# A transformer layer on one core: weight buffers of the first feed-forward layer and residual loads of the second

## The chip, the cores and the metric

The kernel runs on one NeuronCore of a Trainium2 chip, as one launch. The metric is the device time of that launch in microseconds (us). The kernel before takes 2638.78 us, the median of three runs (2638.66 to 2640.82).

## The reference, cut to what matters

One layer of a streaming encoder in fp32, on 2048 new positions and 8 x 16 further ones, 2176 rows of 1024 in all. A projection feeds a gated convolution and a differential attention; the concatenation goes through an output projection and a layer norm. The change concerns only the last two lines:

```python
x1 = layer_norm(ALPHA * x + einsum('bse,ed->bsd', mixed, w_out), ln1_g, ln1_b)
hdn = square(relu(einsum('bsd,df->bsf', x1, w_ff1)))          # first layer, 1024 -> 4096
y = layer_norm(ALPHA * x1 + einsum('bsf,fd->bsd', hdn, w_ff2), ln2_g, ln2_b)   # second, 4096 -> 1024
```

## The kernel before, in words

**Numbers.** Every fp32 product is made of three passes of a reduced type: an operand is split into a high part (a cast on ScalarE, L64) and a low part (a subtraction on VectorE, L67, or on GpSimd), and `mm3` (L71 to L73) adds high x high, low x high (the names in the trace are stationary, moving) and high x low in PSUM. So each operand that TensorE reads is two tiles, h and l, and comes to be by two instructions on two engines.

**First layer.** A Strassen-Winograd scheme takes 2 x 2 blocks with 7 products in place of 8. The 17 row tiles are in three groups of 5, 6 and 6 tiles; a product then has 320 columns in the first group and 384 in the other two. Per group a loop over 16 pairs of column blocks of w_ff1 (`for p in range(NPAIR)`, L1119): the two weight tiles of the pair are loaded (`load_w1`, each 512 KB, into two of the four buffers "raw"), four sums S1 to S4 are formed of them (`w_sources`: the first on GpSimd, L134, three on VectorE), and seven weight operands (11, S1, 12, S2, S3, 22, S4) are split into h and l (`w1_form`). Each of the seven has a place of its own in the pool w1p, with one buffer. `products` makes the 7 products, each 4 x 3 matmuls, and after each product writes the call that forms the same weight for the next pair: it may begin when that product has left the place free. Results go through six PSUM banks, five per pair, through Relu and Square on ScalarE (L1033, L1034) and a few sums, and are stored as seven forms to `hf` in HBM.

**Side work in groups 1 and 2.** Behind some pairs stands work for the next group. `norm_out` (pairs 2, 4, 6, 8, 10, 12) loads a row tile of x1, normalises it and stores it. `turn_out` (pairs 5, 9, 13) loads two such tiles, transposes them on TensorE through four of the six PSUM banks, forms the seven operands T1 and so on, and stores them with seven DMAs (L1113). Its four work tiles, and norm_out's one, are taken from the same four "raw" buffers as the weights. At the end of a group the seven operands of the next group are loaded (L1140) and split. In the third group, which has no such side work, the odd row tile's second layer runs beside the pairs (`odd_prep`, `odd_step`), with buffers wr (two), w2h and w2l of its own.

**Second layer.** Six passes (`PASSES`, L1211) of 16 chunks; a chunk is 24 matmuls of 512 columns. For each chunk a tile of `hf` is loaded to "raw" (`h_load`, L1164, split on ScalarE and VectorE), and one or two quarters of w_ff2 to the places of S1 to S4 (`w_quarter`, L1178, 256 KB), combined on GpSimd in some passes (L1194 to L1200, T = difference of two quarters in the first pass), then split. `prep` does this three chunks ahead. In passes 0, 1, 2 and 5 the residual is prepared: at p == 2 `begin` loads eight halves of x1 to acc tiles (L1259, 256 KB each), and at p = 4 to 11 `residual` multiplies and adds the first norm's gain and bias to one of them on VectorE (L1265, L1266; not for the first group's tiles, whose x1 is stored complete).

**What sets the order.** The program is written in the order of the text, and a scheduler with a simulated timeline then orders each engine's queue: an instruction may move ahead of others on its queue where its operands and buffers allow it. The DMA issues of loads and of most stores share the queue of the sync engine (SP), in one order; a DMA whose buffer is not free waits in that queue with what stands behind it. `tc.issue_after(i)` keeps a DMA behind instruction i.

Of the kernel before, what the change touches and what calls it, by code (L numbers as in the profile page):

```python
# [18 lines left out]
P = 128  # L19
D = 1024  # L20
# [37 lines left out]
def hybrid_layer(ctx: ExitStack, tc: tile.TileContext, A):  # L58
# [82 lines left out]

    def products(N, psum, tmp, X, W, S, form, out, after=None):

        nxt, banks = {}, {}

        def product(xn):
            wn = dict((x, w) for w, x in PRODUCTS)[xn]
            key = {"21": "11", "22": "T1"}.get(xn, xn)  # L150
            more = key in banks
            if not more:
                banks[key] = psum.tile([P, 512], F32, name="pf")[:, :N]
            ps = banks[key]
            for kt in range(4):
                mm3(ps, W[wn][0][:, kt, :], W[wn][1][:, kt, :], X[xn][0][:, kt, :N], X[xn][1][:, kt, :N],
                    kt == 0 and not more, kt == 3, more)
            if wn in S:
                nxt[wn] = form(S, wn)
            if after is not None:  # L160
                after(xn)
            return ps

        u1, u2 = tmp("u1"), tmp("u2")
        for xn in NAMES:
            ps = product(xn)
            if xn == "11":
                nc.scalar.copy(u1, ps)  # L168
            elif xn == "21":
                out(0, 0, ps, True)  # L170
            elif xn == "T2":
                nc.vector.tensor_add(u1, ps, u1)
            elif xn == "T3":
                nc.vector.tensor_add(u2, ps, u1)
                c = tmp("c")
                nc.vector.tensor_add(c, banks["T1"], u2)  # L176
                out(1, 1, c)
            elif xn == "T4":
                c = tmp("c")
                nc.vector.tensor_sub(c, u2, ps)  # L180
                out(1, 0, c)
            elif xn == "22":
                c = tmp("c")
                pin[:] = [nc.vector.tensor_add(c, ps, u1).ins]
                out(0, 1, c)
        return nxt
# [334 lines left out]
    NPAIR = NF // 2  # L521

    loads = []

    def load_w1(p):
        ra, rb = (rwp.tile([P, KT, P], F32, name="raw") for _ in range(2))
        nc.sync.dma_start(ra, A["w_ff1"][p])
        loads.append(nc.sync.dma_start(rb, A["w_ff1"][p + NPAIR]).ins)
        return w_sources(wsp, ra, rb, nc.vector)

    def w1_form(S, nm):
        hl = [w1p.tile([P, 4, P], F32R, name=f"w{nm}{p}") for p in "hl"]
        split(*hl, S[nm], nc.vector)
        return hl


    with ExitStack() as ph:
# [424 lines left out]
        rwp = ffn.enter_context(pool("rwp", 4, side="right"))  # L962
        w1p = ffn.enter_context(pool("w1p", 1, side="right"))
        xtp = xst.enter_context(pool("xtp", 1, side="right"))
# [23 lines left out]
        for i, t in enumerate(ORDER):  # L988
# [11 lines left out]
            if i == 8:  # L1000
                S, W = load_w1(0), {}
                for wn, _ in PRODUCTS:
                    W[wn] = w1_form(S, wn)
# [4 lines left out]
    with ffn as ph:  # L1008
# [8 lines left out]
        def ff1(n, p, X, W, S, at):  # L1017
# [32 lines left out]

            return products(N, ps_f, tmp, X, W, S, w1_form, out)

        def odd_prep(f):

            raw = w2p.tile([P, D], F32, name="wr", bufs=2)
            with tc.issue_after(loads[-1]):
# [9 lines left out]
        def odd_step(f, banks, h, w):  # L1066
            for half in range(2):
                hs = slice(half * 512, half * 512 + 512)
                mm3(banks[half], *h, w[0][:, hs], w[1][:, hs], f == 0, f == NF - 1)

        def norm_out(t):

            r = rwp.tile([P, D], F32, name="xs", tag="raw")
            nc.sync.dma_start(r, x1d[t])
# [12 lines left out]
        def turn_out(gi, i):  # L1087


            a, b = (rwp.tile([P, D], F32, name="xs", tag="raw") for _ in range(2))  # L1090
            for r, t in zip((a, b), groups[gi + 1][i::3]):
                nc.sync.dma_start(r, x1d[t])
            quads = []
            for r in (a, b):
                for g in range(2):
# [3 lines left out]
                    quads.append(ps)  # L1099
            c, d = (rwp.tile([P, D], F32, name="xs", tag="raw") for _ in range(2))  # L1100
            F = {"11": c[:, :512], "21": c[:, 512:], "22": d[:, :512], "T1": a[:, :512], "T2": a[:, 512:],
# [10 lines left out]
            for nm in NAMES:  # L1112
                nc.sync.dma_start(x1f[gi][nm][:, :, i * P:(i + 1) * P], F[nm].rearrange("p (k t) -> p k t", k=4))  # L1113

        couples = [(g[i], g[i + 3]) for g in groups for i in range(len(g) // 2)]
        odd, base, op_, obanks = groups[0][2], 0, None, None
        for gi, tiles in enumerate(groups):
            n, end = len(tiles), gi + 1 == len(groups)
            for p in range(NPAIR):  # L1119
                last = p == NPAIR - 1  # L1120
                S = {} if last and end else load_w1((p + 1) % NPAIR)
                W = ff1(n, p, X, W, S, base * P)
# [30 lines left out]

        def h_load(pieces):

            raw = rwp.tile([P, D], F32, name="hraw", tag="raw")
            for o, src in pieces:
                n = 1
                for k in src.shape[1:]:
                    n *= k  # L1160
                dst = raw[:, o:o + n]
                if len(src.shape) == 3:
                    dst = dst.rearrange("p (k t) -> p k t", k=src.shape[1])
                nc.sync.dma_start(dst, src)  # L1164
            hl = [hrp.tile([P, D], F32R, name="hr" + q) for q in "hl"]
            split(*hl, raw, nc.vector)
            return hl
# [4 lines left out]

        slot = [0]

        def w_quarter(src):
            slot[0] += 1
            a = wsp.tile([P, 512], F32, name="wq", tag=f"wS{slot[0] % 4 + 1}")
            nc.sync.dma_start(a, src)  # L1178
            return a

        def w_load(p, nm):


            rows = {"1": A["w_ff2"][p + NPAIR], "2": A["w_ff2"][p]}

            def quarter(q):
                return w_quarter(rows[q[0]][:, 512 * (q[1] == "2"):512 * (q[1] == "2") + 512])

            if nm in ("T1", "T3"):
                a = quarter("12" if nm == "T1" else "22")  # L1190
                b = quarter("11" if nm == "T1" else "12")
                if nm == "T1":
# [5 lines left out]
            elif nm in ("T2", "T4"):  # L1198
                a = quarter("22" if nm == "T2" else "21")
                nc.gpsimd.tensor_sub(T[p], a, T[p])  # L1200
                a = T[p]
            else:
                a = quarter(nm)
            wn = PRODUCTS[turn_[0] % len(PRODUCTS)][0]
            turn_[0] += 1
            hl = [w1p.tile([P, 512], F32R, name="v" + q, tag=f"w{wn}{q}") for q in "hl"]
            split(*hl, a, nc.vector)
            return hl

        turn_ = [0]  # L1210
        PASSES = (("S1", "T1", None, 2, 1), ("S4", "22", "go", 1, 1), ("11", "11", None, 1, 0), ("S2", "T2", "go", 1, 1),  # L1211
                  ("S3", "T3", "go", 2, 1), ("22", "T4", "go", 2, 0))
        chunks = [(k, p) for k in range(len(PASSES)) for p in range(NPAIR)]

        def prep(k, p):
            hn, wn = PASSES[k][:2]
            return h_load([(0, hf[p][:, FORMS.index(hn), :])]), w_load(p, wn)

# [7 lines left out]

        LEAD = 3
        ready = [prep(*c) for c in chunks[:LEAD]]
        last_odd = rwp.tile([P, D], F32, name="odd", tag="raw")
# [22 lines left out]

        def begin(r, half):
            for c in couples:
                t = c[2 - r]
                if t not in acc:
                    acc[t] = acp.tile([P, D], F32, name=f"acc{t}")
                hs = slice(half * 512, half * 512 + 512)
                nc.sync.dma_start(acc[t][:, hs], x1d[t][:, hs])  # L1259
# [9 lines left out]
        for n, (k, p) in enumerate(chunks):  # L1269
            if n + LEAD < len(chunks):  # L1270
                ready.append(prep(*chunks[n + LEAD]))
            (hh, hl), (wh, wl) = ready.pop(0)
# [3 lines left out]
            if k in (0, 1, 2, 5):  # L1276
                if p == 2:
                    begin(r, half)
                elif 4 <= p < 12:
                    residual(p - 4, r, half)  # L1280
# [12 lines left out]
        def last_w(p):  # L1293
            a = w_quarter(A["w_ff2"][p][:, :512])
            if p < len(PRODUCTS):
                hl = [w1p.tile([P, 512], F32R, name="v" + q, tag=f"w{PRODUCTS[p][0]}{q}") for q in "hl"]
            else:
                hl = [wrp.tile([P, 512], F32R, name=f"z{p}{q}") for q in "hl"]
# [3 lines left out]
        def last_h(q):  # L1302

            if q < 8:
                return h_load([(512 * k, hf[2 * q + k][:, F12, :512]) for k in range(2)])
            i, e = 4 + (q - 8) // 2, (q - 8) % 2
            return h_load([(P * k, hf[8 * e + k][:, F12, i * P:(i + 1) * P]) for k in range(8)])

# [108 lines left out]
```

## Time and profile before

| | us |
|---|---|
| median of three runs | 2638.78 |
| the profiled execution's own time | 2638.29 |
| its span, first to last instruction | 2636.5 |
| TensorE (PE) busy | 2493.7 (95%) |
| VectorE (DVE) busy | 1870.2 (71%) |
| ScalarE (ACT) busy | 1293.2 (49%) |
| GpSimd (POOL) busy | 933.2 (35%) |

[...] The first layer runs from about 1186 to 1986 us of the span (its first pairs among the end of the output projection), the second from 1991 to the end. Busy time is that in which an engine executes; a stretch with TensorE busy can still be slow where the granted clock is low, so matmuls per stretch are counted beside it.

### The profile page before, as it was taken

How to read it: one execution, taken by the hardware profiler on the slowest of the kernel's cores; microseconds unless marked ns; L12 is line 12 of the kernel's file. 1: busy time of each engine (PE TensorE's matmuls, PEld its weight loads, DVE VectorE, ACT ScalarE, POOL GpSimd, SP SyncE). 2: the span in 40 equal slices, each digit the busy share in tenths (PEclk: the TensorE clock that was granted, in tenths of full speed). 3: DMA queues.
4: the chain of work that ended last, by engine and by line, in shares of the span. 5: the costliest groups of instructions: out<-in, count | busy, mean ns of one | idle time of the engine just before them, and what ended most of it. 6: DMA issues, size and time to landing. Idle time of an engine off the chain costs nothing. (4 is left out here: it accounts for less than half of the span.)

```text
span 2636.5 us, 38836 instructions
## 1 busy us (share of the span) xinstructions
PE 2493.7 (95%) x13420; PEld 2257.5 (86%) x13420; DVE 1870.2 (71%) x3103; ACT 1293.2 (49%) x2676; POOL 933.2 (35%) x778
## 2 busy tenths in 40 slices
PE   8999999989999999999997999899998899999998
PEld 7999999968787877789887998899996688888886
DVE  7797676766867777877877777888877634444478
ACT  5444345346666765336665566656553232222231
POOL 5575654655655554221213222322223301314100
PEclk9999999989999999999998999999999899999999
DMA  7437335364535424545766566756668644546444
GB/s 252 157 112 233 111 103 176 86 184 135 158 118 148 141 94 154 181 144 172 229 213 230 188 224 216 286 189 210 213 224 305 207 144 151 167 131 203 144 149 147
DMA packets 273317, 463.24 MB, mean 176 GB/s; under 512 B 32320, under 2 KB 178832, under 8 KB 273120
## 3 DMA queue, kind: packets, MB, share of 16 engines
q1 hardware_dynamic: 260160, 431.58, 50.6%
q10 hardware_dynamic: 11088, 24.12, 2.4%
q0 software_dynamic: 1872, 5.07, 0.6%
q8 instruction: 105, 1.72, 0.3%
q14 instruction: 92, 0.75, 0.1%
HBM read 316.98 MB, written 143.69 MB: 175 GB/s over the span
## 5 line engine op out<-in xcount | busy, mean ns | idle before, releaser
L71 PE MATMUL y<-vh,hrh 128*128 128x512 f32 x824 | 315.8, 394 | 17.5 <-ACT vh L64 17.5
L72 PE MATMUL y<-vl,hrh 128*128 128x512 f32 x824 | 322.0, 391 | 3.2 <-DVE vl L67 3.2
L73 PE MATMUL y<-vh,hrl 128*128 128x512 f32 x824 | 321.4, 390 | 0.0
L67 DVE TENSOR_TENSOR hrl<-hraw,hrh 128x1024 fp32r<-128x1024 f32 x112 | 147.5, 1318 | 214.4 <-ACT hrh L64 214.4
L64 ACT CAST hrh<-hraw 128x1024 fp32r<-128x1024 f32 x112 | 117.9, 1054 | 335.4 <-PE y L72 326.5
L675 ACT ACTIVATE p<-s,nm 128x512 f32<-128x512 f32 (+3 forms) x320 | 199.1, 632 | 96.9 <-DVE nm L673 87.0
L134 POOL TENSOR_TENSOR wS<-raw 128x512 f32<-128x512 f32 x78 | 125.4, 1608 | 314.6 <-DMA raw<-w_ff 174.0
L673 DVE TENSOR_REDUCE nm<-s 128x1 f32<-128x512 f32 (+3 forms) x320 | 184.7, 601 | 41.3 <-PE s L668 39.2
L71 PEld LDWEIGHTS y<-vh,hrh 128*128 128x128 f32 x824 | 156.5, 190 | 51.5 <-ACT vh L64 19.0
L72 PEld LDWEIGHTS y<-vl,hrh 128*128 128x128 f32 x824 | 155.4, 189 | 36.8 <-DVE vl L67 4.3
L73 PEld LDWEIGHTS y<-vh,hrl 128*128 128x128 f32 x824 | 155.4, 189 | 32.4
L702 POOL TENSOR_SCALAR p<-p,cf 128x512 f32<-128x512 f32 (+3 forms) x160 | 123.8, 793 | 148.7 <-DVE cf L695 122.9
L667 PE MATMUL s<-kt,aq 128*128 128x512 f32 (+3 forms) x344 | 137.0, 406 | 16.2 <-DMA kt<-k_sc 9.2
L751 PE MATMUL pa<-a,vt 128*128 128x256 f32 (+1 forms) x576 | 140.7, 371 | 0.4 <-ACT a L730 0.4
L71 PE MATMUL pf<-x11h,w11h 128*128 128x384 f32 (+1 forms) x324 | 110.8, 342 | 25.5 <-ACT w11h L64 13.6
L668 PE MATMUL s<-kt,ql 128*128 128x512 f32 (+3 forms) x344 | 124.3, 369 | 0.6 <-DMA ql<-q_sc 0.6
L71 PE MATMUL pf<-x21h,w12h 128*128 128x384 f32 (+1 forms) x324 | 109.0, 336 | 9.5 <-ACT u L168 9.5
L751 PEld LDWEIGHTS pa<-a,vt 128*128 128x128 f32 x576 | 104.3, 191 | 14.5 <-ACT a L730 1.2
L71 PE MATMUL pf<-x22h,wS4h 128*128 128x384 f32 (+1 forms) x324 | 108.7, 335 | 7.7 <-DVE c L176 7.7
L71 PE MATMUL pf<-xT1h,wS1h 128*128 128x384 f32 (+1 forms) x324 | 107.6, 332 | 7.2 <-ACT wS1h L64 6.2
L1200 POOL TENSOR_TENSOR t<-wq,t 128x512 f32<-128x512 f32 x32 | 52.1, 1645 | 167.6 <-DMA wq<-w_ff 167.4
L73 PE MATMUL pf<-xT1h,wS1l 128*128 128x384 f32 (+1 forms) x324 | 107.6, 332 | 3.8 <-DVE wS1l L67 3.8
(652 smaller groups left out, 7870.7 us busy)
## 6 DMA issues: line engine op xcount, KB each, us to landing
raw<-w_ff SPq DMA_DIRECT2D x96, 512.0 KB, 4.1
hraw<-hf SPq DMA_DIRECT2D x96, 512.0 KB, 3.9
wq<-w_ff SPq DMA_DIRECT2D x144, 256.0 KB, 3.7
raw<-w_in SPq DMA_DIRECT2D x70, 512.0 KB, 4.2
hf<-h SPq DMA_DIRECT2D x32, 768.0 KB, 3.7
wr<-w_ff SPq DMA_DIRECT2D x32, 512.0 KB, 3.5
xs<-x1d SPq DMA_DIRECT2D x24, 512.0 KB, 5.0
hf<-h SPq DMA_DIRECT2D x32, 384.0 KB, 2.5
```

The costliest lines, as they stand in the source:

```text
L64: nc.scalar.copy(hi, src)
L67: return lo_eng.tensor_sub(lo, src, hi)
L71: nc.tensor.matmul(ps, lh, rh, start=start, stop=False, skip_group_check=more)
L72: nc.tensor.matmul(ps, lh, rl, start=False, stop=False, skip_group_check=more)
L73: nc.tensor.matmul(ps, ll, rh, start=False, stop=stop, skip_group_check=more)
L134: nc.gpsimd.tensor_add(S["S1"], a21, a22)
L667: nc.tensor.matmul(ss[c][:, pos:pos + m], aq[:, c, qsl], kt[:, c], start=True, stop=False)
L668: nc.tensor.matmul(ss[c][:, pos:pos + m], ql[:, c, qsl], kt[:, c], start=False, stop=True)
L673: nc.vector.tensor_reduce(nm[:, qb, ci, c:c + 1], s[:, :kn], axis=AX.X, op=ALU.max, negate=True)
L675: nc.scalar.activation(pt[:, :kn], s[:, :kn], AF.Exp, bias=nm[:, qb, ci, c:c + 1], accum_out=sm[:, qb, ci, c:c + 1])
L702: nc.gpsimd.tensor_scalar(p1[:, :kn], p1[:, :kn], X["cf"][:, qb, ci, 1:2], 1.0, op0=ALU.mult, op1=ALU.mult)
L751: nc.tensor.matmul(o, vt[:, kb % 4, :], a[:, i], start=first, stop=end)
```

## The change

In the first layer a rotating ring of eight places takes over from the seven named ones, and one form runs ahead (`lead`). Weights are loaded two pairs ahead, with the sums made one pair ahead as before. norm_out and turn_out take the odd tile's buffers. In the second layer the loads of the first two chunks stand in the text before the last pair; `begin` loads one half per chunk (p = 1 to 8), each kept behind the newest load of an hf tile. `h_load` and `w_load` become a loading part (`raws2`) and a forming part (`h_form`, `w_form`).

```diff
-    def products(N, psum, tmp, X, W, S, form, out, after=None):
+    def products(N, psum, tmp, X, W, S, form, out, after=None, lead=0):
...
-            if wn in S:
-                nxt[wn] = form(S, wn)
+            ahead(NAMES.index(xn) + lead)
...
+        def ahead(i):
+            if i < len(PRODUCTS) and PRODUCTS[i][0] in S:
+                nxt[PRODUCTS[i][0]] = form(S, PRODUCTS[i][0])
+
+        for i in range(lead):
+            ahead(i)
...
+    RING = 8
...
     def load_w1(p):
-        ra, rb = (rwp.tile([P, KT, P], F32, name="raw") for _ in range(2))
-        nc.sync.dma_start(ra, A["w_ff1"][p])
-        loads.append(nc.sync.dma_start(rb, A["w_ff1"][p + NPAIR]).ins)
-        return w_sources(wsp, ra, rb, nc.vector)
+        raws = [rwp.tile([P, KT, P], F32, name="raw") for _ in range(2)]
+        for j, raw in enumerate(raws):
+            loads.append(nc.sync.dma_start(raw, A["w_ff1"][p + NPAIR * j]).ins)
+        return raws
+
+    def sums_w1(raws):
+        return w_sources(wsp, *raws, nc.vector)
 
     def w1_form(S, nm):
-        hl = [w1p.tile([P, 4, P], F32R, name=f"w{nm}{p}") for p in "hl"]
+        hl = [w1p.tile([P, 4, P], F32R, name=f"w{nm}{p}", tag="w" + p) for p in "hl"]
...
-        w1p = ffn.enter_context(pool("w1p", 1, side="right"))
+        w1p = ffn.enter_context(pool("w1p", RING, side="right"))
...
-            return products(N, ps_f, tmp, X, W, S, w1_form, out)
+            return products(N, ps_f, tmp, X, W, S, w1_form, out, lead=RING - len(PRODUCTS))
...
-            raw = w2p.tile([P, D], F32, name="wr", bufs=2)
+            raw = w2p.tile([P, D], F32, name="wr", tag=f"wr{f % 2}")
...
+        def spare(tag):
+            return w2p.tile([P, D], F32, name="xs", tag=tag)
...
-            r = rwp.tile([P, D], F32, name="xs", tag="raw")
+            r = spare(f"wr{t % 2}")
...
-            a, b = (rwp.tile([P, D], F32, name="xs", tag="raw") for _ in range(2))
+            a, b = spare("wr0"), spare("wr1")
...
-            c, d = (rwp.tile([P, D], F32, name="xs", tag="raw") for _ in range(2))
+            c, d = spare("w2h"), spare("w2l")
...
+        EARLY, LEAD = 2, 3
...
+        def raws2(k, p):
+            hn, wn = PASSES[k][:2]
+            return (h_raw([(0, hf[p][:, FORMS.index(hn), :])]),
+                    [w_quarter(A["w_ff2"][p + NPAIR * (q[0] == "1")][:, 512 * (q[1] == "2"):512 * (q[1] == "2") + 512])
+                     for q in QUARTERS.get(wn, (wn,))])
...
+        raws = load_w1(1)
         for gi, tiles in enumerate(groups):
             n, end = len(tiles), gi + 1 == len(groups)
             for p in range(NPAIR):
                 last = p == NPAIR - 1
-                S = {} if last and end else load_w1((p + 1) % NPAIR)
+                S = {} if last and end else sums_w1(raws)
+                if not end or p < NPAIR - 2:
+                    raws = load_w1((p + 2) % NPAIR)
+                if last and end:
+                    early = [raws2(*c) for c in chunks[:EARLY]]
                 W = ff1(n, p, X, W, S, base * P)
...
-            wn = PRODUCTS[turn_[0] % len(PRODUCTS)][0]
-            turn_[0] += 1
-            hl = [w1p.tile([P, 512], F32R, name="v" + q, tag=f"w{wn}{q}") for q in "hl"]
+            hl = [w1p.tile([P, 512], F32R, name="v" + q, tag="w" + q) for q in "hl"]
...
-        LEAD = 3
-        ready = [prep(*c) for c in chunks[:LEAD]]
+        ready = [prep(*c, r) for c, r in zip(chunks, early)]
...
-        def begin(r, half):
-            for c in couples:
-                t = c[2 - r]
-                if t not in acc:
-                    acc[t] = acp.tile([P, D], F32, name=f"acc{t}")
-                hs = slice(half * 512, half * 512 + 512)
+        def begin(i, r, half):
+            t = couples[i][2 - r]
+            if t not in acc:
+                acc[t] = acp.tile([P, D], F32, name=f"acc{t}")
+            hs = slice(half * 512, half * 512 + 512)
+            with tc.issue_after(hloads[-1]):
                 nc.sync.dma_start(acc[t][:, hs], x1d[t][:, hs])
...
-            if n + LEAD < len(chunks):
-                ready.append(prep(*chunks[n + LEAD]))
+            for c in chunks[n + len(ready):n + LEAD + 1]:
+                ready.append(prep(*c, raws2(*c)))
...
-                if p == 2:
-                    begin(r, half)
-                elif 4 <= p < 12:
+                if 1 <= p < 9:
+                    begin(p - 1, r, half)
+                if 4 <= p < 12:
                     residual(p - 4, r, half)
```

## Rows read from the trace of the kernel before

**Rows 1.** Page, part 1: busy time, share of the span, instructions of TensorE.

```profile
PE 2493.7 (95%) x13420; PEld 2257.5 (86%) x13420; DVE 1870.2 (71%) x3103; ACT 1293.2 (49%) x2676; POOL 933.2 (35%) x778
```

**Rows 2.** Stretches: length, each engine's busy time, instructions; granted clock, DMA share, GB/s.

```profile
1850.00:1900.00 50.00, 50.00 (x279) 48.60 (x278) 42.88 (x63) 30.70 (x59) 12.26 (x9) 1.00 0.61 209
```

**Rows 3.** Stretches of groups 1 and 2; engines in the order PE, PEld, DVE, ACT, POOL.

```profile
1364.00:1376.00 12.00, 12.00 (x84) 12.00 (x83) 9.73 (x20) 8.91 (x19) 3.19 (x3) 1.00 0.88 297
1274.00:1289.00 15.00, 11.70 (x63) 10.24 (x62) 11.50 (x22) 11.17 (x24) 4.00 (x4) 0.89 1.00 320
1333.00:1350.00 17.00, 11.17 (x62) 9.95 (x61) 10.57 (x22) 10.98 (x22) 4.80 (x4) 0.90 0.94 309
1392.00:1407.00 15.00, 10.87 (x61) 9.92 (x60) 10.45 (x17) 9.26 (x20) 4.12 (x4) 0.89 1.04 337
1539.00:1556.00 17.00, 13.01 (x62) 11.73 (x61) 14.55 (x23) 10.53 (x22) 5.45 (x4) 0.90 0.75 258
1607.00:1624.00 17.00, 10.78 (x51) 10.13 (x50) 14.71 (x24) 10.83 (x22) 6.18 (x4) 0.80 0.71 253
1673.00:1692.00 19.00, 15.22 (x67) 14.04 (x66) 13.85 (x19) 10.71 (x20) 5.84 (x4) 0.82 0.85 279
1513.00:1526.00 13.00, 10.54 (x58) 10.15 (x57) 10.31 (x17) 7.28 (x17) 1.56 (x2) 0.87 0.41 147
1455.00:1475.00 20.00, 20.00 (x116) 19.66 (x115) 15.95 (x32) 12.59 (x27) 4.61 (x4) 1.00 0.57 198
```

**Rows 4.** Timeline of SP around a turn: start, time in queue's issue, line, DMA.

```profile
1332.64 1.24 SPq L1113 DMA_DIRECT2D x1fT<-xs  x2
1333.93 0.65 SPq L527 DMA_DIRECT2D raw<-w_ff  x1
```

**Rows 5.** Timeline of TensorE: start, time, line, product; in brackets idle before and releaser.

```profile
1339.70 0.41 PE L71 MATMUL pf<-x11h,w11h 128*128 128x320 f32 x1 [4.59 <-ACT w11h L64]
```

**Rows 6.** Waits of ScalarE, 1190 to 1990: us in total, times, longest.

```profile
ACT wS4h L64 <- PE pf L72: 37.0, 23, 3.1
...
ACT w11h L64 <- DMA raw<-w_ff: 19.4, 7, 6.6
```

**Rows 7.** Stretches at the two changes of group.

```profile
1407.00:1440.00 33.00, 21.40 (x105) 19.63 (x104) 22.48 (x26) 19.04 (x26) 9.46 (x6) 0.84 0.66 234
1692.00:1725.00 33.00, 26.48 (x124) 24.07 (x123) 33.00 (x33) 21.22 (x31) 16.57 (x6) 0.90 0.85 330
```

**Rows 8.** Stretches of the second layer: its start, two more, an undisturbed one.

```profile
1985.00:2000.00 15.00, 9.54 (x32) 6.61 (x31) 13.18 (x18) 5.87 (x9) 7.54 (x8) 0.77 0.80 282
2012.00:2034.00 22.00, 22.00 (x99) 18.03 (x98) 17.91 (x23) 6.70 (x8) 8.15 (x4) 1.00 1.03 393
2034.00:2062.00 28.00, 14.21 (x46) 10.79 (x45) 25.55 (x38) 3.34 (x4) 14.13 (x4) 0.70 0.77 272
2100.00:2200.00 100.00, 100.00 (x443) 82.81 (x442) 41.29 (x51) 28.32 (x36) 0.00 (x0) 1.00 0.46 143
```

**Rows 9.** Timeline of TensorE at the first change of group.

```profile
1415.34 0.61 PE L71 MATMUL pf<-x22h,wS4h 128*128 128x320 f32 x1 [4.07 <-DVE c L176]
1423.87 0.69 PE L71 MATMUL pf<-x11h,w11h 128*128 128x384 f32 x1 [5.06 <-ACT x11h L64]
```

**Rows 10.** Waits of SP's queue, 1200 to 1990.

```profile
SPq L528 <- DVE w22l L67: 63.6, 22, 12.0
```

**Rows 11.** Tile acc: ns min/median/max, first and last start, forms.

```profile
L1259 SPq DMA_DIRECT2D acc<-x1d x32: 319/320/857, 2007.6 to 2041.9; - x32
...
L1265 DVE TENSOR_TENSOR acc<-acc,gb x24: 677/682/1779, 2014.5 to 2057.8; 128x512 f32<-128x512 f32 x24
```

**Rows 12.** Timeline of GpSimd in the first pass of the second layer.

```profile
2006.97 1.28 POOL L1194 TENSOR_TENSOR t<-wq 128x512 f32<-128x512 f32 x1 [0.24 <-DMA wq<-w_ff]
...
2045.29 10.18 POOL L1194 TENSOR_TENSOR t<-wq 128x512 f32<-128x512 f32 x1 [12.35 <-DMA wq<-w_ff]
```

**Rows 13.** Timeline of SP before the second layer.

```profile
1944.76 4.12 SPq L1164 DMA_DIRECT2D hraw<-hf  x2
```

More of the change, by code (lines that the diff above doesn't have):

```diff
@@ L1000, in hybrid_layer @@
             if i == 8:
-                S, W = load_w1(0), {}
+                S, W = sums_w1(load_w1(0)), {}
                 for wn, _ in PRODUCTS:
@@ L1113, in turn_out, with h_raw, w_quarter @@
                 nc.sync.dma_start(x1f[gi][nm][:, :, i * P:(i + 1) * P], F[nm].rearrange("p (k t) -> p k t", k=4))
+        EARLY, LEAD = 2, 3
+        hloads = []
+        def h_raw(pieces):
+            raw = rwp.tile([P, D], F32, name="hraw", tag="raw")
+            for o, src in pieces:
+                n = 1
+                for k in src.shape[1:]:
+                    n *= k
+                dst = raw[:, o:o + n]
+                if len(src.shape) == 3:
+                    dst = dst.rearrange("p (k t) -> p k t", k=src.shape[1])
+                hloads.append(nc.sync.dma_start(dst, src).ins)
+            return raw
+        slot = [0]
+        def w_quarter(src):
+            slot[0] += 1
+            a = wsp.tile([P, 512], F32, name="wq", tag=f"wS{slot[0] % 4 + 1}")
+            nc.sync.dma_start(a, src)
+            return a
+        PASSES = (("S1", "T1", None, 2, 1), ("S4", "22", "go", 1, 1), ("11", "11", None, 1, 0), ("S2", "T2", "go", 1, 1),
+                  ("S3", "T3", "go", 2, 1), ("22", "T4", "go", 2, 0))
+        chunks = [(k, p) for k in range(len(PASSES)) for p in range(NPAIR)]
+        QUARTERS = {"T1": ("12", "11"), "T2": ("22",), "T3": ("22", "12"), "T4": ("21",)}
+        def raws2(k, p):
[3 more added lines that the diff above has]
+                     for q in QUARTERS.get(wn, (wn,))])
         couples = [(g[i], g[i + 3]) for g in groups for i in range(len(g) // 2)]
         odd, base, op_, obanks = groups[0][2], 0, None, None
+        raws = load_w1(1)
         for gi, tiles in enumerate(groups):
@@ L1152, in hybrid_layer, with h_form @@
         tst = ExitStack()
[L1154 to L1164, printed above, removed]
+        def h_form(raw):
             hl = [hrp.tile([P, D], F32R, name="hr" + q) for q in "hl"]
@@ L1171, in hybrid_layer, with w_form @@
         ttp = tst.enter_context(pool("ttp", 1, side="right"))
[L1173 to L1187, printed above, removed]
+        def w_form(p, nm, raw):
+            a = raw[0]
             if nm in ("T1", "T3"):
-                a = quarter("12" if nm == "T1" else "22")
-                b = quarter("11" if nm == "T1" else "12")
+                b = raw[1]
                 if nm == "T1":
@@ L1198, in w_load @@
             elif nm in ("T2", "T4"):
-                a = quarter("22" if nm == "T2" else "21")
                 nc.gpsimd.tensor_sub(T[p], a, T[p])
                 a = T[p]
-            else:
-                a = quarter(nm)
-            wn = PRODUCTS[turn_[0] % len(PRODUCTS)][0]
-            turn_[0] += 1
-            hl = [w1p.tile([P, 512], F32R, name="v" + q, tag=f"w{wn}{q}") for q in "hl"]
+            hl = [w1p.tile([P, 512], F32R, name="v" + q, tag="w" + q) for q in "hl"]
             split(*hl, a, nc.vector)
             return hl
[L1210 to L1217, printed above, removed]
         gains = []
@@ L1225, in hybrid_layer, with prep @@
         gain = gains[1]
-        LEAD = 3
-        ready = [prep(*c) for c in chunks[:LEAD]]
+        def prep(k, p, raw):
+            return h_form(raw[0]), w_form(p, PASSES[k][1], raw[1])
+        ready = [prep(*c, r) for c, r in zip(chunks, early)]
         last_odd = rwp.tile([P, D], F32, name="odd", tag="raw")
@@ L1294, in last_w @@
             a = w_quarter(A["w_ff2"][p][:, :512])
-            if p < len(PRODUCTS):
-                hl = [w1p.tile([P, 512], F32R, name="v" + q, tag=f"w{PRODUCTS[p][0]}{q}") for q in "hl"]
+            if p < RING:
+                hl = [w1p.tile([P, 512], F32R, name="v" + q, tag="w" + q) for q in "hl"]
             else:
@@ L1304, in last_h @@
             if q < 8:
-                return h_load([(512 * k, hf[2 * q + k][:, F12, :512]) for k in range(2)])
+                return h_form(h_raw([(512 * k, hf[2 * q + k][:, F12, :512]) for k in range(2)]))
             i, e = 4 + (q - 8) // 2, (q - 8) % 2
-            return h_load([(P * k, hf[8 * e + k][:, F12, i * P:(i + 1) * P]) for k in range(8)])
+            return h_form(h_raw([(P * k, hf[8 * e + k][:, F12, i * P:(i + 1) * P]) for k in range(8)]))
         def norm2(t):
```

## The prediction

> **What bounds the kernel now.** I read the page's busy times first. TensorE works 2493.7 us of a 2636.5 us span [rows 1]. So TensorE is the bound and what can be won is its idle and half-clock time; the question is where that lies. Next came a table of stretches over the second half. In the last third of the first layer a 50 us stretch has TensorE busy all 50 us at full clock, with VectorE at 42.88 us [rows 2]: the layer's own work, the odd tile's included, fits under the matmuls when nothing else disturbs it. The same table cut narrowly around TensorE's gaps gives the losses [rows 3]. A loss is the stretch less its matmuls at the undisturbed rate. The rate is 12.00/84, with the cut ends some 0.146 us, for 320 columns (first group), and 20.00/116 = 0.172 us for 384 (second). [...] Sum 44.8 us.
> The queue's timeline shows what the first six share: each follows a turn_out. The turn takes all four "raw" buffers; the next pair's weights are issued only behind its last x1f stores, at 1333.93, and TensorE runs dry at 1335.1 [rows 4]. The first product starts at 1339.70, after 4.59 us in which TensorE waits for the cast of w11 [rows 5], and ScalarE's cast of w11 waits for the landing, seven times in the layer and 19.4 us in all [rows 6]. The seventh is the same buffers a little earlier: the second half of a weight pair waits for a place.
> Then come the two changes of group, 16 us (33 - 105 x about 0.162, both widths in it) and 11.7 us (33 - 124 x 0.172) [rows 7], and the start of the second layer. There 1985-2000 loses 15 - 32 x 0.226 = 7.8 us and 2034-2062 loses 28 - 46 x 0.226 = 17.6 us, against 443 matmuls in 100 us when it runs clean [rows 8]. All of it together is about 98 us.
>
> **The change part by part.**
> *Weights alone in their buffers, two pairs ahead.* norm_out and turn_out move to the odd tile's buffers, which nothing uses in groups 1 and 2. No instruction is added: per pair still 2 loads, 4 sums and 7 splits, 16 transposes per turn. A load now has about one pair more (84 x 0.146 = 12.3 us, or 84 x 0.172 = 14.5 us). The weights came at most 4.59 us late in [rows 5], and with the backlog behind it the worst stretch lost 8.2 us [rows 3]. One pair covers that, so I take the whole 44.8 us. What is late next in those pairs: VectorE, busy 42.88 of 50 us in the last group and without a stall there [rows 2]. So the cover is thin, not gone. Bounds: 0 (the x1f stores or the turn's use of the PSUM banks hold the pair as well) to -44.8.
> *Groups' changes.* The loads of the next group's operands stay, and so does their traffic. The 5.06 us of idle time at 1423.87 waits for x11h; that is not touched. But the 4.07 us at 1415.34 waits for VectorE, which at that point is still working off two pairs' splits that came late from the turn before [rows 9]. I take half of the first change, 8 us, and nothing of the second. Bounds 0 to -27.7.
> *One more operand place.* The eight places go round; the split for product i+1 of the next pair takes the place that product i leaves, one product (12 x 0.172 = 2.1 us) earlier than its need required before. What it adds is a coupling: a weight waits for another product than its own. ScalarE then stands at the cast, with Relu and Square queued behind it and the PSUM banks behind these. Such waits exist already, for S4 alone 37.0 us in 23 times, the longest 3.1 us [rows 6], and the last group, which has them too, is without a gap [rows 2]. Bounds, over 48 pairs: nothing below 0, since the slack helps only in the gaps counted above; up to 3.1 us per pair, 149 us, if each pair met the longest wait bare. I take 0.1 us per pair, +5 us, an estimate close to the row without a gap.
> *Loads two ahead on SP.* Each load's place was left by the pair before it. SP has waited for such a place 22 times, 63.6 us in all, up to 12.0 [rows 10]. If a load were to stand in SP before its place is free, the hf stores behind it stand too, and with two buffers of results the Relu. Its last reader of that pair, the seventh split, runs before the pair ends, so I take 0; bounds -2 to +5.
> [...]
> *Residual loads, one per chunk.* Before, all 32 acc loads (256 KB each) went out between 2007.6 and 2041.9, although begin is called in four passes; with them went the residual's multiplications and additions, up to 2057.8 [rows 11]. Two things follow. DMA is full (1.03 at 393 GB/s in 2012-2034 [rows 8]), so that GpSimd waits 12.35 us for a quarter of the weights; and its subtraction at 2045.29 then takes 10.18 us where one took 1.28 us before [rows 12], because VectorE runs its two-operand work back to back beside them. TensorE waits for their result. After the change a chunk (24 x 0.226 = 5.4 us) has one load and at most two such operations (2 x 0.68 = 1.4 us). The load is three chunks, 16 us, ahead of its use. I take the whole 17.6 us of 2034-2062. Bounds 0 to -19.6 (with a 2 us gap at 2005).
> [...]
> *First chunks loaded early.* The scheduler has already put them there: two hraw at 1944.76, 40 us before the layer [rows 13]. So this part is 0. The third chunk is no longer among the early ones by the program's order: -2 to +6 us (the loss of 1985-2000, once more in part). The start itself waits for the first layer's operands to be freed and for GpSimd, and stays: 7.8 us.
> Sum: -44.8 - 8 + 5 + 0 - 17.6 + 0 = -65.4 us. The profiled execution took 2638.29 us (span 2636.5 and 1.8 around it) and the median of three is 2638.78, 0.5 more: 2638.8 - 65.4 = 2573.4, call it 2574.
>
> **The rivals.**
> A. Only part of the first layer's stalls goes: the turn's stores and its four PSUM banks of six hold the pair as the buffers did. For it: VectorE at 86% leaves little to catch up with. Against: stretches without a turn, [rows 3] first and last, are full. Then a third of 44.8 and the 17.6: -33 us, 2606.
> B. The changes of group and the second layer's start go too, since their backlog comes from the same late weights: -65.4 - 27 = -92, 2546. For: the 4.07 us. Against: the next operands still have to be loaded, with DMA at 0.85 in the second change [rows 7].
> C. Slower. The shared places: ScalarE's queue stands at a cast whose place belongs to a product that TensorE runs late, and this empties the PSUM rotation in each of 48 pairs. It turns the gain around from 65.4 + 5 = 70 us, 1.47 us per pair; at 1.9 us per pair it costs 91, so 2569 + 91 = 2660. For: such waits average 37.0/23 = 1.6 us. Against: they leave no gap today, and one product of slack is added.
> D. It doesn't do what it says: the scheduler orders the loads by its own times and puts them behind the turn again, and the residual work still in one heap. Then the time stays, 2638, within 0.2% (5.3 us, about what a measurement of this kernel can tell).
>
> **How the numbers follow.** Forecast 0.56, A 0.19, B 0.10, C 0.08, D 0.07. Faster by over 0.2%: the first three and a little of D, 0.86; within: 0.05; slower: C and a little of D, 0.09. The forecast's own bounds: the group change 0 to -16 and the coupling 0 to +20 make 2561 to 2597. For eight in ten the range must take in A with its spread up to 2618 and part of B down to 2550.
>
> **What would show it.** [...] acc loads spread over four passes, no subtraction of GpSimd over 4 us in the first pass, and no 11.76 us gap. A gap at the start of the second layer stays, and one at each change of group. Wrong: gaps behind turn_out with the weights already there (A), regular small gaps in every pair of group 3, which had none (C), or a first pass of the second layer with waits for hraw or wq.

## The result and the profile after

The changed kernel takes 2572.1 us, the median of four runs (2571.7 to 2574.1), beside 2639.8 us for four runs of the kernel before: a ratio of 0.9744 with a 95% interval of 0.9727 to 0.9761. The forecast was 2574 in 2550 to 2618. The profiled execution took 2571.69 us, its span is 2569.9, and the mean granted clock is 0.986.

The page of the kernel after, part 1, answers to [rows 1]:

```profile
PE 2469.0 (96%) x13420; PEld 2243.4 (87%) x13420; DVE 1877.1 (73%) x3103; ACT 1291.4 (50%) x2676; POOL 914.0 (36%) x778
```

The instruction counts are the same and no engine has less to do; TensorE's busy time falls by 25 us with the granted clock up from 0.977 to 0.986: less of its work runs at half clock. The granted clock is 1.00 in the microsecond from 1390 us of the span before, and 0.50 in the one from 1399 us. Where the rest went shows in the stretches of the first layer after, cut around turns of group 1 (the first two rows) and of group 2 (the fourth and fifth) and around both changes of group (the third and the last); they answer to [rows 3, 7]. A row gives the window, its length, the busy time and instructions of PE, PEld, DVE, ACT and POOL, then the granted clock, the DMA share and GB/s:

```profile
1254.00:1276.00 22.00, 22.00 (x156) 21.98 (x155) 15.94 (x26) 17.46 (x42) 5.20 (x5) 1.00 0.58 180
1357.00:1383.00 26.00, 25.59 (x178) 25.34 (x178) 21.97 (x38) 20.10 (x49) 6.94 (x6) 1.00 0.83 259
1390.00:1424.00 34.00, 21.11 (x99) 19.61 (x98) 24.72 (x39) 24.70 (x38) 8.73 (x6) 0.75 0.94 344
1545.00:1575.00 30.00, 30.00 (x181) 29.93 (x180) 23.33 (x36) 19.70 (x45) 8.39 (x6) 1.00 0.62 199
1605.00:1636.00 31.00, 31.00 (x187) 30.93 (x186) 24.49 (x38) 20.75 (x47) 8.43 (x6) 1.00 0.64 207
1645.00:1690.00 45.00, 39.17 (x208) 37.19 (x207) 42.96 (x48) 28.97 (x47) 17.91 (x8) 0.96 0.74 263
```

Behind the turns TensorE is full at clock 1.00: 187 matmuls in 31 us is 0.166 us each, where such a stretch took 17 us for 51 [rows 3]. In SyncE's queue the next pair's weights now go out ahead of the turn's first store, where they stood behind its last [rows 4]:

```profile
1317.88 0.33 SPq L536 DMA_DIRECT2D raw<-w_ff  x1
1319.18 0.53 SPq L1128 DMA_DIRECT2D x1f<-xs  x1
```

In ScalarE's waits after, w11h waits for no load any more (seven times and 19.4 us before [rows 6]).

The two changes of group remain. By the prediction's rates the first loses 34 - 99 x 0.162 = 18.0 us (16 before) and the second 45 - 208 x 0.172 = 9.2 (11.7 before). A second profiled execution of the same kernel, from the last experiment below, has 93 and 195 matmuls in these two windows, a loss of 18.9 and 11.5 us. So the first change got no better, and the second is not shown to have moved. TensorE's timeline after shows what changed in the first one; the rows of before are [rows 9]:

```profile
1395.81 0.41 PE L71 MATMUL pf<-x22h,wS4h 128*128 128x320 f32 x1 [1.06 <-DVE c L182]
1406.99 0.69 PE L71 MATMUL pf<-x11h,w11h 128*128 128x384 f32 x1 [9.16 <-ACT x11h L64]
```

The wait ahead of x22 fell from 4.07 to 1.06 us, and the wait for x11h grew from 5.06 to 9.16. Together they were 9.13 us and are 10.22: nothing was won at this place, a wait was exchanged for another. In four more profiled executions below, with these loads and eight places, the wait for x11h is 8.9 to 9.3 us.

What grew in it shows on ScalarE, which casts x11 to its high part. The first row is before, the other two after:

```profile
1422.35 1.47 ACT L64 CAST x11h<-x11l 128x1536 fp32r<-128x1536 f32 x1 [2.00 <-DMA x11l<-x1f]
1405.46 1.47 ACT L64 CAST x11h<-x11l 128x1536 fp32r<-128x1536 f32 x1 [3.70 <-DMA x11l<-x1f]
1398.11 1.24 ACT L1099 ACTIVATE xs<-xs,sh,rs 128x1024 f32<-128x1024 f32 x1
```

ScalarE stands idle for the load 2.00 us before and 3.70 after. So 1.7 of the 4.1 us are a later load, and the other 2.4 are work of ScalarE's own, a step of norm_out (L1099) and a weight's cast among it, that now stands between the group's last product and this cast.

In the second layer the stretches after answer to [rows 8], its start in the first two rows, the first pass in the third:

```profile
1937.00:1952.00 15.00, 9.14 (x33) 6.57 (x32) 12.59 (x18) 6.14 (x9) 7.81 (x8) 0.89 0.78 275
1952.00:1966.00 14.00, 12.10 (x46) 9.51 (x46) 8.89 (x8) 3.87 (x5) 4.52 (x3) 0.88 0.94 323
1966.00:2014.00 48.00, 48.00 (x213) 39.74 (x213) 32.35 (x35) 17.22 (x23) 15.63 (x11) 1.00 0.86 294
```

The first pass is full at 0.225 us per matmul. The start loses 15 - 33 x 0.226 = 7.5 and then 14 - 46 x 0.226 = 3.6 us. Windows in the same places of the kernel before lose 15 - 34 x 0.226 = 7.3 us (1986 to 2001) and 14 - 53 x 0.226 = 2.0 us:

```profile
2001.00:2015.00 14.00, 11.95 (x53) 9.59 (x52) 7.33 (x8) 4.42 (x6) 4.75 (x3) 1.00 0.93 326
```

The residual's tile acc after, answering to [rows 11], has its 32 loads spread over 451 us instead of 34:

```profile
L1281 SPq DMA_DIRECT2D acc<-x1d x32: 320/424/913, 1959.7 to 2410.8; - x32
```

GpSimd's subtractions in this pass, with [rows 12] as their counterpart, take 1.28 to 2.33 us, with a median of 1.34; one of them:

```profile
1970.34 1.29 POOL L1228 TENSOR_TENSOR t<-wq 128x512 f32<-128x512 f32 x1 [5.73 <-DMA wq<-w_ff]
```

**The account.** The second layer's first product starts at 1991.08 us before and at 1943.33 after:

```profile
1991.08 2.50 PE L71 MATMUL y<-vh,hrh 128*128 128x512 f32 x5 [3.69 <-ACT vh L64]
```

(that is TensorE before), and after, with a later wait of the start:

```profile
1943.33 3.41 PE L71 MATMUL y<-vh,hrh 128*128 128x512 f32 x8 [3.71 <-ACT vh L64]
1959.56 3.56 PE L71 MATMUL y<-vh,hrh 128*128 128x512 f32 x8 [1.91 <-ACT vh L64]
```

So 47.75 us of the span's 66.6 were won up to that product, and from there to the end 645.42 - 626.57 = 18.85 us.

### The profile page after: what moved, and what is told of

Read it like the earlier page. It is cut to its first block, busy times and chain, and to the rows that moved or that the text cites. A ratio compares the mean times of both kernels' runs of the same rounds, so it can differ in the third digit from the quotient of the medians.

```text
span 2569.9 us, 38835 instructions
## 1 busy us (share of the span) xinstructions
PE 2469.0 (96%) x13420; PEld 2243.4 (87%) x13420; DVE 1877.1 (73%) x3103; ACT 1291.4 (50%) x2676; POOL 914.0 (36%) x778
## 5 line engine op out<-in xcount | busy, mean ns | idle before, releaser
L71 PE MATMUL y<-vh,hrh 128*128 128x512 f32 x832 | 323.1, 393 | 5.6 <-ACT vh L64 5.6
L134 POOL TENSOR_TENSOR wS<-raw 128x512 f32<-128x512 f32 x78 | 113.6, 1457 | 166.2 <-DVE wS1l L67 100.4
L72 PE MATMUL pf<-x11l,w11h 128*128 128x384 f32 (+1 forms) x324 | 108.4, 335 | 1.1 <-DVE x11l L67 1.1
L73 PE MATMUL pf<-x11h,w11l 128*128 128x384 f32 (+1 forms) x324 | 107.8, 333 | 0.0
```

What stands on the lines that cost most here:

```text
L71: nc.tensor.matmul(ps, lh, rh, start=start, stop=False, skip_group_check=more)
L72: nc.tensor.matmul(ps, lh, rl, start=False, stop=False, skip_group_check=more)
L73: nc.tensor.matmul(ps, ll, rh, start=False, stop=stop, skip_group_check=more)
L134: nc.gpsimd.tensor_add(S["S1"], a21, a22)
```

## The experiments

Each was timed beside the kernel before on the same chip, on three chips in all, so that runs of different chips compare by their ratios. The theory: two independent gains, the weights' own buffers (some 45 us) and the spread residual (some 17 us); the ring and the lead of the loads bring nothing. The rivals put part of it into the lead or the ring.

**Only other buffers for the side work** (the kernel before, norm_out and turn_out on the odd tile's buffers):

```diff
-            raw = w2p.tile([P, D], F32, name="wr", bufs=2)
+            raw = w2p.tile([P, D], F32, name="wr", tag=f"wr{f % 2}")
...
+        def spare(tag):
+            return w2p.tile([P, D], F32, name="xs", tag=tag)
...
-            r = rwp.tile([P, D], F32, name="xs", tag="raw")
+            r = spare(f"wr{t % 2}")
...
-            a, b = (rwp.tile([P, D], F32, name="xs", tag="raw") for _ in range(2))
+            a, b = spare("wr0"), spare("wr1")
...
-            c, d = (rwp.tile([P, D], F32, name="xs", tag="raw") for _ in range(2))
+            c, d = spare("w2h"), spare("w2l")
```

> The kernel before, with one edit: norm_out and turn_out take the odd tile's buffers; weights still one pair ahead, named operand places, residual burst as before. Theory (the stalls behind turn_out come of the shared raw buffers alone): the six stretches behind the turns are full, about 45 us less than before, 2594 us. Rival (a load must also come a pair earlier, or it still lands late behind the turn's x1f stores on SP): gaps of 2 to 5 us stay behind the turns, gain 10 to 25 us, 2615 to 2630.

Measured: 2594.5 us beside 2640.0, ratio 0.9829 (0.9814 to 0.9845). Its stretches, nearly all of group 1 and of group 2, and the place of the burst:

```profile
1250.00:1370.00 120.00, 116.64 (x802) 115.50 (x801) 98.85 (x184) 85.82 (x195) 29.34 (x26) 1.00 0.72 234
1430.00:1655.00 225.00, 223.09 (x1303) 222.31 (x1302) 188.17 (x292) 147.20 (x307) 61.08 (x45) 1.00 0.64 219
1998.00:2012.00 14.00, 1.24 (x5) 0.72 (x4) 12.20 (x20) 1.74 (x3) 10.94 (x2) 0.64 0.73 271
```

The turns' stalls are gone in group 2 (225 - 1303 x 0.172 leaves under 1 us) and nearly so in group 1 (120 - 802 x 0.146 leaves 2.9 us, where two turns lost 13.7). The burst's gap stays. TensorE at the first change of group:

```profile
1396.90 0.41 PE L71 MATMUL pf<-x22h,wS4h 128*128 128x320 f32 x1 [3.20 <-DVE c L176]
1409.14 0.69 PE L71 MATMUL pf<-x11h,w11h 128*128 128x384 f32 x1 [9.47 <-ACT x11h L64]
```

The longer wait for x11h comes with these buffers alone, without ring or lead. The rival, that weights must also be written a pair earlier, falls. With the buffers free the loads run ahead of the text by themselves: when the 17th of the 48 pairs starts, 37 loads have gone out here and 38 in the kernel after, where 34 are needed.

**Loads one pair ahead** (the kernel after):

```diff
-        raws = load_w1(1)
...
-                S = {} if last and end else sums_w1(raws)
-                if not end or p < NPAIR - 2:
-                    raws = load_w1((p + 2) % NPAIR)
+                S = {} if last and end else sums_w1(load_w1((p + 1) % NPAIR))
```

> The changed kernel with the weights loaded one pair ahead again; own buffers, eight places and the second layer stay changed. Theory: the lead of loads is worth nothing once the buffers are alone, 2572 within 5 us, since the scheduler moves the loads forward to where their buffers come free. Rival: the second pair of lead carries part of the 45 us, 2585 to 2600.

Measured: 2572.5 us, ratio 0.9748 (0.9730 to 0.9766), within the interval of the kernel after. But the edit moved hardly anything. Here are a weight load and the first product of a pair in group 2, after and then in this run:

```profile
1470.62 0.36 SPq L536 DMA_DIRECT2D raw<-w_ff  x1
1470.82 0.33 PE L71 MATMUL pf<-x11h,w11h 128*128 128x384 f32 x1
```

```profile
1466.68 0.36 SPq L536 DMA_DIRECT2D raw<-w_ff  x1
1466.88 0.33 PE L71 MATMUL pf<-x11h,w11h 128*128 128x384 f32 x1
```

In both the load goes out 0.20 us ahead of the product. So the scheduler had put the loads there already. The run shows that the lead in the text brings nothing; what a load that truly goes out a pair later would cost, no run shows.

**Seven places** (the kernel after, `RING = 7`):

> The changed kernel with seven operand places and no form ahead (each weight then has its own product's place again). Theory: the eighth place neither costs the 5 us that the prediction set for the coupling nor brings anything, 2572 within 4 us. Rival: one product of slack closes the small gaps of 0.4 to 1 us that are gone from groups 1 and 2, so without it the time rises by 5 to 10 us, 2577 to 2582.

Measured: 2574.2 us, ratio 0.9753 (0.9735 to 0.9771): no difference that shows. At the first change of group it waits 7.41 us for x11h in place of 9.16, at the second 8.29 us for x21l.

**Only the residual spread** (the kernel before, one acc load per chunk):

```diff
...
-                nc.sync.dma_start(dst, src)
+                hloads.append(nc.sync.dma_start(dst, src).ins)
...
-        def begin(r, half):
-            for c in couples:
-                t = c[2 - r]
...
+        def begin(i, r, half):
+            t = couples[i][2 - r]
...
+            with tc.issue_after(hloads[-1]):
                 nc.sync.dma_start(acc[t][:, hs], x1d[t][:, hs])
...
-                if p == 2:
-                    begin(r, half)
+                if 1 <= p < 9:
+                    begin(p - 1, r, half)
```

> The kernel before, with one edit: the residual's loads one per chunk, each kept behind the newest hf load; first layer as before. Theory: the 11.76 us gap in the first pass goes with the burst, about 18 us less than before, 2621 us. Rival: the second layer gains only because the first layer ends differently (loads early): 2635 to 2640, gap stays.

Measured: 2623.8 us, ratio 0.9934 (0.9916 to 0.9952). One of the old stretches behind turns and the second layer's first 100 us:

```profile
1607.00:1624.00 17.00, 10.30 (x46) 9.67 (x45) 13.10 (x20) 10.92 (x21) 5.97 (x4) 0.80 0.88 314
2010.00:2110.00 100.00, 99.72 (x440) 82.58 (x441) 60.47 (x71) 33.03 (x44) 18.70 (x13) 1.00 0.74 246
```

The turns stall as before, the burst's gap is gone. The two parts gain 45.5 and 16.2 us, 61.7 of the 67.7; what is between lies within the three intervals. The two together, without ring and lead, were not run.

**What spreads the residual** (the kernel after, without the pin):

```diff
-            with tc.issue_after(hloads[-1]):
-                nc.sync.dma_start(acc[t][:, hs], x1d[t][:, hs])
+            nc.sync.dma_start(acc[t][:, hs], x1d[t][:, hs])
```

> The changed kernel, with the residual loads still written one per chunk but no longer pinned behind a raw load of the second layer. Theory (the pin is what spreads them, since loads without it are moved to the earliest moment at which the buffers are free): all 32 are issued together at the second layer's start again, the gap of 11 to 13 us in TensorE's work there returns, and the time is 2585 to 2591 us. Rival (their place in the text is enough): no gap, 2571 to 2574 us.

Measured: 2586.2 us, ratio 0.9790 (0.9765 to 0.9815). The tile acc in this run:

```profile
L1280 SPq DMA_DIRECT2D acc<-x1d x32: 319/320/758, 1959.0 to 1991.2; - x32
```

and GpSimd in the first pass:

```profile
1994.55 12.01 POOL L1228 TENSOR_TENSOR t<-wq 128x512 f32<-128x512 f32 x2 [10.55 <-DMA wq<-w_ff]
```

With one load per chunk in the text and no pin, all 32 go out in 32 us again, and GpSimd again takes 12.01 us for two subtractions. The pin is what spreads them. TensorE then waits 1.43, 3.04 and 7.72 us; the last of these:

```profile
2006.03 3.78 PE L71 MATMUL y<-vh,hrh 128*128 128x512 f32 x8 [7.72 <-ACT vh L64]
```

**The second layer's start** (the kernel after, the two early chunks formed ahead of the gain loads in the text):

```diff
+        ready = [prep(*c, r) for c, r in zip(chunks, early)]
         gains = []
...
         gain = gains[1]
-        ready = [prep(*c, r) for c, r in zip(chunks, early)]
```

> The changed kernel, with the gain and bias loads on GpSimd's queue written behind the first two chunks' forms instead of ahead of them. Theory (the 3.7 us gap at the second layer's start comes from GpSimd, which issues those loads first and only then makes the differences for the first operands): GpSimd starts its differences 2 us earlier, and the time is 2569 to 2570.5 us. Rival (GpSimd waits for the buffers of the first layer's last operands, or the gap is set by another wait): 2571.5 to 2573 us, gap unchanged.

Measured: 2566.1 us, ratio 0.9712 (0.9691 to 0.9732). TensorE of this run, then GpSimd after and GpSimd of this run:

```profile
1937.61 3.34 PE L71 MATMUL y<-vh,hrh 128*128 128x512 f32 x8 [2.54 <-ACT vh L64]
```

```profile
1939.20 0.55 POOL L1243 DMA_DIRECT2D gb<-ln_g  x1
...
1941.35 3.55 POOL L1228 TENSOR_TENSOR t<-wq 128x512 f32<-128x512 f32 x2
```

```profile
1934.65 3.48 POOL L1228 TENSOR_TENSOR t<-wq 128x512 f32<-128x512 f32 x2
```

After, four of these issues stand ahead of GpSimd's first differences and hold them for 2.15 us; here the differences come first, and TensorE's wait at the start falls from 3.71 to 2.54 us. It is 2.52 us in the two later runs with this edit and 3.68 to 3.71 us in every run without it. From the first product to the end the span has 623.3 us instead of 626.6; the three runs with the edit have 623.0 to 623.6 us, the five that have the pin and the early loads but not this edit 625.3 to 627.6. That is some 4.5 us by place. The wait of 1.91 us a chunk later is gone too, but without the edit it is only 0.20 us with seven places and 0.26 us in the next run, so its loss can't be put down to the edit. The profiled execution is 9.0 us shorter than that of the kernel after; the other 4.5 us of it lie ahead of the edit. As the interval meets that of the kernel after, the sum itself is not settled, and the 2569 to 2570.5 us expected were missed.

**The change of group** (the kernel after, the seven operand loads on GpSimd's queue):

```diff
-                        nc.sync.dma_start(raw, x1f[gi][nm])
+                        nc.gpsimd.dma_start(raw, x1f[gi][nm])
```

> The changed kernel, with the seven loads of the next group's operands (x11 to x22, twice in the kernel) issued on GpSimd's queue instead of SyncE's. Theory (they are late because SyncE's queue is in order and they stand behind loads and stores that wait for VectorE and ScalarE, while their buffers come free one by one from some 14 us before the group's last product): x11l is issued 5 to 14 us earlier against the last product, the gap of 9.2 us at the first change of group falls to under 4 us, the second change gains some 2 to 4 us too, and the time is 2558 to 2566 us. Rival (the buffers come free only with the group's last product, so the queue costs little): the issue moves by 1 us at most and the time is 2570 to 2573 us. Second rival (GpSimd, blocked at these loads, is late with its sums and stalls TensorE): 2573 us or more.

Measured: 2569.0 us, ratio 0.9723 (0.9699 to 0.9746): not told apart from the kernel after, and the wait came down less than the "under 4 us" expected. At the place itself the mechanism shows. SyncE's queue in the kernel before:

```profile
1417.38 0.37 SPq L1140 DMA_DIRECT2D x11l<-x1f  x1
```

the same queue after, with what stands ahead of x11l:

```profile
1398.46 0.33 SPq L536 DMA_DIRECT2D raw<-w_ff  x1
1398.89 0.37 SPq L1197 DMA_DIRECT2D x11l<-x1f  x1
```

and in this run GpSimd's queue, with what it does next:

```profile
1389.66 0.55 POOL L1197 DMA_DIRECT2D x11l<-x1f  x1
...
1412.39 1.27 POOL L134 TENSOR_TENSOR wS<-raw 128x512 f32<-128x512 f32 x1 [12.68 <-DMA raw<-w_ff]
1413.62 3.42 POOL L67 TENSOR_TENSOR xT3l<-xT3l,xT3h 128x1536 fp32r<-128x1536 f32 x1
```

TensorE there:

```profile
1399.81 0.69 PE L71 MATMUL pf<-x11h,w11h 128*128 128x384 f32 x1 [5.34 <-ACT x11h L64]
...
1417.10 0.69 PE L72 MATMUL pf<-xT3l,wS3h 128*128 128x384 f32 x1 [4.55 <-POOL xT3l L67]
```

Reckoned from the end of the group's last product (the start of the x11 product less its wait), x11l is issued 1.4 us ahead of it in the kernel before, 1.06 us behind it after (1398.89 against 1397.83), and 4.8 us ahead of it here. The wait falls from 9.16 to 5.34 us, and is 5.34 and 5.32 us in the two later runs with this edit. What is left of it is no load's. ScalarE's cast follows on other work without idle time:

```profile
1398.31 1.46 ACT L64 CAST x11h<-x11l 128x1536 fp32r<-128x1536 f32 x1
```

The 3.8 us won are about the 3.70 us for which ScalarE stood idle after. But 4.55 us come back: GpSimd's queue has the first sum of the next pair ahead of the low part of xT3, and this sum waits 12.68 us for weights. So GpSimd is late as in the second rival, though held by the weights and not by the operand loads. A gain at the second change of group, also expected, doesn't show: 218 matmuls in its 45 us, beside 208 and 195 in the two executions of the kernel after.

**Both, and both with xT3 on VectorE**, with the kernel after once more on the same chip:

```diff
-                        split(hi, lo, raw, nc.gpsimd if nm in ("T3", "T4") else nc.vector)
+                        split(hi, lo, raw, nc.gpsimd if nm == "T4" else nc.vector)
```

> The changed kernel itself, unaltered, so that the next two are compared with it on one chip: 2569 to 2575 us by every theory.

> Both edits together: gain and bias loads behind the first chunks' forms, and the next group's operand loads on GpSimd's queue. Theory (the two act at different places and add: 6 and 3 us below the changed kernel): 2561 to 2565 us. Rival (what either gives is within the scatter from chip to chip): 2568 us or more, within 4 us of the changed kernel run beside it.

> As the run before, with the difference of xT3 made by VectorE (1.76 us each) instead of GpSimd (3.42 us), since that difference was late at the first change and left a gap of 4.6 us. Theory (it is late because GpSimd makes a sum of the next pair's weights first, which waits for a load): the gap falls to 1 to 2 us and the time is 2 to 4 us under the run before. Rival (the group's change is bound by DMA, which moves 5.4 MB of operands beside the weights, so another operand is late in its place): within 1 us of the run before.

Measured: the kernel after 2570.3 us, ratio 0.9740 (0.9725 to 0.9756); both edits 2564.8, ratio 0.9722 (0.9708 to 0.9735); with xT3 on VectorE 2557.0, ratio 0.9690 (0.9671 to 0.9709). Both edits alone lie 5.4 us under the kernel after with intervals that overlap. The last lies clear below the kernel after: 13 us faster, and 82 faster than the one before, the fastest version here. Against the run with both edits its interval only just touches; it is 7.8 us faster by the medians, where 2 to 4 were expected, and 3.7 by the profiled spans (2559.2 and 2562.9). TensorE at both its changes of group:

```profile
1402.94 0.69 PE L71 MATMUL pf<-x11h,w11h 128*128 128x384 f32 x1 [5.32 <-ACT x11h L64]
...
1662.77 0.69 PE L72 MATMUL pf<-xT3l,wS3h 128*128 128x384 f32 x1 [3.50 <-DVE xT3l L67]
```

The gap at xT3l of the first change is gone (5.48 us with both edits) and no other operand is late in its place, so there DMA is not the bound. At the second change the same operand is late instead, by 3.50 us, where the run with both edits had no such wait: VectorE has the work there now. The remaining 5.32 us, ScalarE's, were not pursued.

## Why the prediction was right, and where it was not

*The seven stretches, -44.8.* Right, in place and size: the stretches are full, and the buffers alone gave 45.5 us. Of [rows 3] the second to the eighth, at 0.146 us a matmul in group 1 and 0.172 in group 2, give 5.8, 7.9, 6.1, 6.3, 8.2, 7.5 and 3.0 us, idle time and half clock in one number. The pair more of time for a load, with which the prediction argued the full size, comes from the free buffers, not from the new order of the text: that run keeps the old order. The view that carried it was SP's queue, with the next pair's loads behind the turn's stores [rows 4].

*Change of group, -8.* This step failed. The wait that it named went (4.07 to 1.06 us). But the prediction also said of the wait for x11h that it "is not touched", and it grew by 4.1 us. With the pair no longer late, TensorE comes to the end of the group earlier against two queues. In SP's, x11l stands behind stores and loads with waits of their own; issuing it elsewhere brought the wait to 5.34 us, so 3.8 of the 9.16 are the load's. In ScalarE's, the cast of x11 stands behind other work; the rest of the wait lies there, read from the timeline and not tested by an edit. The first change lost 16 us and loses 18 to 19.

*The ring, +5.* It did not come. ScalarE's waits for places did, in a table of waits of the kernel after that answers to [rows 6]:

```profile
ACT wS3h L64 <- PE pf L72: 49.8, 32, 3.0
ACT wS1h L64 <- PE pf L72: 46.6, 21, 12.1
```

Both were shorter before (11.5 and 7.9 us); the one for S4 fell from 37.0 to 24.6. No wait of TensorE for a weight's cast stands behind them: between the changes of group it waits 1.1 us in all in group 1, for VectorE, and the list of its waits is empty for groups 2 and 3. Seven places take the same time. So rival C has nothing in it, and the ring no use here. Two errors cancel: for both changes -8 was taken and for the ring +5; +2.0 and -2.5 were found at the changes (+2.9 and -0.2 in the second execution) and nothing for the ring.

*Loads two ahead, 0.* Right in size, but because the scheduler issues the loads at the same moments either way, which the prediction said of the second layer's first chunks and not here. The wait of SP that stood for it [rows 10] is still there, at no cost:

```profile
SPq L536 <- DVE w22l L67: 66.9, 33, 10.2
```

*The residual, -17.6.* Right; alone it gave 16.2 us, and after it no subtraction of GpSimd in the first pass takes over 2.33 us. That the spread hangs on the pin, not on the place in the text, the prediction had not said. Its two causes, full DMA (1.03 [rows 8]) and a subtraction of 10.18 us beside VectorE's two-operand work [rows 12], come and go together with the burst, and no run has one without the other; the rows in the last section part them, by an estimate, for the longest wait.

*First chunks early, 0 within -2 to +6.* The start lost 7.3 + 2.0 us and loses 7.5 + 3.6: +1.8, inside the bounds. The part from the first product of the second layer to the end gained 18.85 us where -17.6 was taken.

The total, -65.4 against -66.6 measured in the profiled executions, is closer than its steps, and that is luck in part. Found by place are -44.8, -0.5 at the changes, 0 for the ring, +1.8 at the start and -17.6: -61.1 us. The other 5.5 us lie in no stretch shown here. Rivals A and D fall with the full stretches. Rival B had a point: the changes of group and the start do hold time, 13 us of it by the medians within three small edits, but it did not go with the late weights.

## What to carry to other kernels

When a stall goes, read the next deadline on the queues that serve it: the engine now arrives earlier, and a load or a cast that was just in time becomes the wait. Where a scheduler places DMAs by free buffers, moving a load in the text may move nothing; check its issue times before an equal time is called an answer, and hold it by a dependency where it must move. A gap is judged with its neighbours: 4.07 and 5.06 became 1.06 and 9.16.

## What the hardware showed that was not expected

GpSimd's 128x512 subtraction took 1.28 us for one and 10.18 us for another in [rows 12], and 12.01 us for two in the run without the pin, the long ones beside VectorE's two-operand work (a median of 682 ns in [rows 11], 678 in that run). In the kernel after, most of the rows show 1.28 to 1.9 us, one 2.33. The 10.18 us go with a whole run of VectorE's operations, not with one of them: before, VectorE's run without idle time ends with this row, and TensorE then starts:

```profile
2051.86 2.49 DVE L1266 TENSOR_TENSOR acc<-acc,gb 128x512 f32<-128x512 f32 x4
2056.18 3.78 PE L71 MATMUL y<-vh,hrh 128*128 128x512 f32 x8 [11.76 <-ACT vh L64]
```

The run ends at 2054.35 and the subtraction at 2055.47, 1.1 us later, about the 1.28 us of the short one. That VectorE's work holds the subtraction off is read from these times; no run shows it apart from the burst.

Full DMA alone does not account for it. From 2050 to 2056 the DMA share is 0.36, and GpSimd is still busy throughout. In the kernel after, one subtraction took 1.79 us with the DMA share at 0.96 and VectorE busy for 0.74 us:

```profile
2050.00:2056.00 6.00, 0.00 (x0) 0.00 (x0) 4.35 (x8) 0.49 (x1) 6.00 (x2) 0.50 0.36 104
```

```profile
1957.00:1959.00 2.00, 0.66 (x3) 0.20 (x2) 0.74 (x1) 0.11 (x1) 1.79 (x1) 1.00 0.96 385
```

At 1.28 us the subtraction would have ended 8.9 us sooner. So, as an estimate from these rows, 8.9 of TensorE's 11.76 us are the long subtraction and 2.9 the late load of the weights.
